# Attention values in halves of 64 queries, with the mixed corners corrected on quarters of the matmul array

## The chip, the core and the metric

The kernel runs on one NeuronCore of one Trainium2 chip. Its engines work side by side, each with its own queue: TensorE (PE in the profile, with PEld for loading its stationary operands, the "weights"), VectorE (DVE), ScalarE (ACT), GpSimd (POOL) and SyncE (SP). The last two mainly issue DMAs here. TensorE writes its results to PSUM, and VectorE and ScalarE read them from there.

The metric is the time of one launch in device microseconds (us). The median of three runs of the kernel before is 2309.34 us.

## The reference

One inference step of a two-layer decoder of width 2048 in fp32: a prompt of 1024 tokens, and eight single tokens that are decoded against caches. The first layer is a pooling mixer, the second one attention over a sliding window of 128 keys. The change touches the prompt's attention alone:

```python
def attn_core(q, k, v, q_pos, k_pos, sinks):
    s = jnp.einsum('...qkgd,...skd->...kgqs', q, k).astype(jnp.float32) * (HEAD_DIM ** -0.5)
    qp = q_pos[..., :, None]
    kp = k_pos[..., None, :]
    mask = (kp <= qp) & (qp - kp < WINDOW) & (kp >= 0)
    s = jnp.where(mask[..., None, None, :, :], s, NEG)
    ...
    p = jnp.exp(s - m)
    p = p / (jnp.sum(p, axis=-1, keepdims=True) + jnp.exp(sink - m))
    return jnp.einsum('...kgqs,...skd->...qkgd', p.astype(v.dtype), v)
```

Queries and keys go in blocks of 128 (`WINDOW`). Query number r of a block sees keys 0 to r of its own block and keys r+1 to 127 of the block before. So each query sees 128 keys, and for each key number k just one of the two blocks: its own where k <= r, else the one before. There are 32 query heads of width 64 on four key/value heads.

## The kernel before

**Steps.** Nearly all of the time goes into large products: the projections into and out of the two layers. Every fp32 operand is split into a rounded high part and a low remainder, and three matmuls (L684, L685, L686: high by high, high by low, low by high) make one product. Weights come in blocks of 128 x 1024; seven blocks in Strassen's scheme give two 128-row tiles of the result. One block is one *step*: 24 matmuls with 128 x 128 weights and 256 or 260 moving columns. (In a few places a step is half a unit of L712 to L714, 12 matmuls of 512 columns.)

**What sets the order.** The order of instructions on TensorE, VectorE and ScalarE is that of the source, written out by hand (`in_order`). A counter `i` goes up by one at the end of each step, and the attention's work hangs on it: `product(n, rank, go)` puts TensorE work at the end of step i+n, behind that step's 24 matmuls and sorted by rank; `at(n, go)` puts work of other engines there, behind the products. Between these, VectorE and ScalarE split the weights of coming steps (L505 on ScalarE, L520 on VectorE) and take results out of PSUM. `side_step` runs pieces of side work (layer norm, sums of weights), and passes where `lastO` says that the one-bank PSUM tile `pO` was taken just then.

**Attention.** The prompt goes in two chunks of 512 queries (c = 0, 1; chunk 1 also carries the eight decode tokens), that is NB = 4 query blocks each. `attend(c, t, ...)` is called for t = 0 to 15 in each chunk, 32 calls; one call does two heads (j = 0, 1, on partitions 0 to 63 and 64 to 127) for the four blocks. Its parts, some steps apart:

- `score` (PE, L1878): 32 fp32 matmuls with weights of 64 rows x 32 columns and 160 moving keys, into the four-bank PSUM tile `pS` (`self.S`, 2 x 1024 columns, one half for each j). The profile shows two records for each fp32 matmul.
- `select` (ACT, L1895) and `largest` (DVE, L1899) put the scores on the two key blocks into one 128 x 128 array per head and block; then come exponents, sums and the norm (L1914 to L1927).
- `turn` (PE, L1931): eight transposes into the first half of `pS`.
- `keep`: a copy `w` (ACT, L1940) and a masked copy `wp` (DVE, L1941) that keeps only entries with k > r.
- `values` (PE, L1955): for each block and head, all 128 keys of `w` against the own block's values `V[b + 1]`, and all 128 keys of `wp` against `Vd[b]`, the values of the block before less the own ones. These are 16 fp32 matmuls of 128 rows x 64 columns with 128 moving queries. They go to `pO` for t up to 12, to the second half of `pS` for t = 13 to 15.
- `gate` (DVE, L1964): the multiplication by the gate, out of PSUM, and a DMA of the result (POOL, L1967).

Calls start every seven steps. `phase_bi` gives each its place: `at` is the step of `score`, s1 the steps from there to `turn`, s2 = 2 those from `turn` to `values`; `gate` follows one step later. For most calls s1 is 12, so the values of one call fall to the end of the same step as the score of the next call but one, and rank puts the values first.

The decode tokens have small matmuls of their own: L2049 (weights of 64 rows x 128 columns, 8 moving columns) and L2089 (128 rows x 64 columns, 8 moving columns).

## Time and profile before

| | |
|---|---|
| three runs, median (lowest to highest) | 2309.34 us (2308.86 to 2309.92) |
| profiled execution: span from first to last instruction | 2308.8 us |
| TensorE busy | 2286.2 us (99%) |
| VectorE, ScalarE busy | 1943.5 us (84%), 1389.0 us (60%) |
| first score to last gate of the prompt's attention | 1148 to 2004 us of the span |

The profiled execution's own time is known by its span; the three runs lie 0.1 to 1.1 us above it.

A timeline row has start and duration in us, engine, line, operation, output and inputs, the part of the array in use (rows * columns), partitions x moving columns, and the number of records joined in the row. Matmuls are pipelined and their ends are modelled, so the distance from one start to the next says more of a matmul's cost than its duration. Matmuls on different parts of the array can run side by side: then several start within a few ns.

### The profile page before, as it was taken

The page shows a single profiled execution, that of the slowest core. Times are in us where ns is not written, and L with a number is a line of the kernel's source. Part 1 is how long each engine was busy: PE and PEld are TensorE (multiplying, and loading weights), DVE is VectorE, ACT ScalarE, POOL GpSimd, SP SyncE. Part 2 cuts the span into 40 slices and gives each one's busy share as a digit, 9 for nine tenths or more (in the row PEclk, how much of TensorE's full clock was granted, in tenths as well). Part 3 has the DMA queues.
Part 4 walks back from the last instruction along what each step waited for, and adds up shares of the span by engine and source line. Part 5 has one row for each costly group of instructions (what it writes and reads, how often), then busy time and mean ns, then how long its engine had stood idle before and what let it go on. Part 6 is the DMA issues. An engine that isn't in the chain of part 4 may idle for free.

```text
span 2308.8 us, 50518 instructions
## 1 busy us (share of the span) xinstructions
PE 2286.2 (99%) x20417; PEld 2216.1 (96%) x20417; DVE 1943.5 (84%) x2415; ACT 1389.0 (60%) x2547; POOL 191.1 (8%) x359
## 2 busy tenths in 40 slices
PE   9999999999999999999999999999999999999998
PEld 7999999999999999999889999999999999999998
DVE  8888889877868878998878888999877777888997
ACT  5544446544546556555576766785776678656665
POOL 0111100010000000000001111100000000000001
PEclk9999999999999999999999999999999999999999
DMA  7879679988989989999767667777787778799894
GB/s 260 284 245 315 229 252 327 317 302 300 303 304 323 339 293 321 317 385 359 235 241 249 224 237 243 263 273 233 236 261 233 248 241 293 245 365 360 286 342 149
DMA packets 246395, 648.31 MB, mean 281 GB/s; under 512 B 25201, under 2 KB 106001, under 8 KB 246161
## 3 DMA queue, kind: packets, MB, share of 16 engines
q1 hardware_dynamic: 204288, 493.13, 63.7%
q0 software_dynamic: 41872, 151.96, 17.0%
q8 instruction: 159, 2.61, 0.5%
q14 instruction: 76, 0.61, 0.1%
HBM read 463.00 MB, written 172.47 MB: 275 GB/s over the span
## 4 chain that ended last, share of the span: by engine, by line
PE 56%; DVE 1%; DMA 1%; ACT 0%; issue 0%; POOL 0%; SPq 0%; DVEq 0%; POOLq 0%
PE pD L684 15%; PE pD L686 14%; PE pD L685 14%; PE pO L1955 2%; PE pD L712 2%; PE pD L714 2%; PE pD L713 2%; PE pS L1878 2%; PE pS L1931 1%; DMA m<-in_wob 0%; PE pS L1955 0%; PE pO L684 0%; PE pO L685 0%; PE pO L686 0%; DVE m L520 0%; DMA m<-in_wib 0%
## 5 line engine op out<-in xcount | busy, mean ns | idle before, releaser
L684 PE MATMUL pD<-m,m 128*128 128x260 f32 (+1 forms) x5088 | 1441.1, 283 | 4.4 <-ACT pD L623 2.2
L686 PE MATMUL pD<-m,m 128*128 128x260 f32 (+1 forms) x5088 | 1434.0, 282 | 5.8 <-DVE m L520 5.8
L685 PE MATMUL pD<-m,m 128*128 128x260 f32 (+1 forms) x5088 | 1434.2, 282 | 0.0
L684 PEld LDWEIGHTS pD<-m,m 128*128 128x128 f32 x5088 | 958.9, 188 | 13.7 <-issue 6.2
L686 PEld LDWEIGHTS pD<-m,m 128*128 128x128 f32 x5088 | 959.5, 189 | 7.6 <-DVE m L520 7.4
L685 PEld LDWEIGHTS pD<-m,m 128*128 128x128 f32 x5088 | 958.6, 188 | 0.5
L520 DVE TENSOR_TENSOR m<-m,m 128x1024 fp32r<-128x1024 f32 x690 | 834.1, 1219 | 94.4 <-ACT m L505 37.9
L505 ACT CAST m<-m 128x1024 fp32r<-128x1024 f32 x690 | 720.6, 1049 | 247.5 <-DVE m L349 122.4
L349 DVE TENSOR_TENSOR m<-m,m 128x1024 f32<-128x1024 f32 x136 | 166.2, 1222 | 8.6 <-DMA m<-in_wia 5.6
L847 DVE TENSOR_TENSOR m<-m,m 128x1024 fp32r<-128x1024 f32 (+1 forms) x118 | 144.0, 1225 | 7.4 <-ACT m L838 5.8
L838 ACT CAST m<-m 128x1024 fp32r<-128x1024 f32 (+1 forms) x118 | 123.3, 1051 | 8.3 <-DVE m L520 3.9
L657 ACT COPY m<-pD 128x260 f32<-128x260 f32 (+1 forms) x88 | 32.9, 374 | 125.8 <-PE pD L686 125.6
L645 DVE TENSOR_TENSOR m<-pD,m 128x260 f32<-128x260 f32 (+1 forms) x92 | 38.3, 417 | 74.3 <-ACT pD L644 68.2
L1914 ACT ACTIVATE m<-m,sm 128x128 f32<-128x128 f32 x256 | 99.4, 392 | 0.0
L623 ACT ACTIVATE pD<-pD 128x260 f32<-128x260 f32 (+1 forms) x90 | 33.3, 370 | 98.8 <-PE pD L686 98.4
L1181 PE MATMUL pD<-m,m 128*128 128x260 f32 (+1 forms) x528 | 91.5, 323 | 0.0
L712 PE MATMUL pD<-m,m 128*128 128x512 f32 x224 | 89.1, 398 | 0.0
L714 PE MATMUL pD<-m,m 128*128 128x512 f32 x224 | 88.2, 394 | 0.0
L713 PE MATMUL pD<-m,m 128*128 128x512 f32 x224 | 88.1, 393 | 0.0
L1181 PEld LDWEIGHTS pD<-m,m 128*128 128x128 f32 x528 | 79.4, 188 | 8.2
L1927 ACT ACTIVATE m<-m,sm 128x128 f32<-128x128 f32 x256 | 81.9, 391 | 7.8 <-DVE sm L1922 7.2
L632 ACT COPY m<-pD 128x260 f32<-128x260 f32 (+1 forms) x92 | 34.4, 374 | 82.6 <-PE pD L686 82.4
(257 smaller groups left out, 2102.7 us busy)
## 6 DMA issues: line engine op xcount, KB each, us to landing
m<-in_wib SPq DMA_DIRECT2D x132, 512.0 KB
m<-in_wia SPq DMA_DIRECT2D x128, 512.0 KB
m<-swoa SPq DMA_DIRECT2D x64, 512.0 KB
swia<-m POOLq DMA_DIRECT2D x56, 512.0 KB, 4.8
m<-swia SPq DMA_DIRECT2D x56, 512.0 KB
m<-swob SPq DMA_DIRECT2D x56, 512.0 KB
m<-in_wob SPq DMA_DIRECT2D x52, 512.0 KB
m<-in_woa SPq DMA_DIRECT2D x48, 512.0 KB
```

The source lines that it names most:

```text
L349: self.nc.vector.tensor_add(s[out].a[:, :1024], s[x].a[:, :1024], s[y].a[:, :1024])
L505: self.nc.scalar.copy(hi.r[:, :1024], self.stream[self.cast].src().a[:, :1024])
L520: self.nc.vector.tensor_sub(lo.r[:, :1024], s.src().a[:, :1024], hi.a[:, :1024])
L684: nc.tensor.matmul(ps[:, :TH], wh[:, s], h, start=new and k == 0, stop=False, skip_group_check=on)
L685: nc.tensor.matmul(ps[:, :TH], wh[:, s], l, start=False, stop=False, skip_group_check=on)
L686: nc.tensor.matmul(ps[:, :TH], wl[:, s], h, start=False, stop=k == 7, skip_group_check=on)
L712: nc.tensor.matmul(ps[:], wh[:, s], h, start=par == 0 and k == 0, stop=False)
L713: nc.tensor.matmul(ps[:], wh[:, s], l, start=False, stop=False)
L714: nc.tensor.matmul(ps[:], wl[:, s], h, start=False, stop=par == 1 and k == 7)
L838: self.nc.scalar.copy(h.r[:, :n], s.a[:, :n])
L847: self.nc.vector.tensor_sub(l.r[:, :n], s.a[:, :n], h.a[:, :n])
L1181: nc.tensor.matmul(ps[:, : cs.stop - cs.start], ws[:, s], d[:, cs], start=f0 and k == 0, stop=l0 and k == 3,)
```

## The change

For queries 0 to 63 of a block (u = 0), keys 64 to 127 can only be those of the block before; for queries 64 to 127 (u = 1), keys 0 to 63 can only be the own ones. `values` now takes each half of 64 queries with all 128 keys against one block's values (`V[b]` for u = 0, `V[b + 1]` for u = 1). Only a corner of 64 keys by 64 queries is mixed, and is corrected with `Vd[b]` by matmuls of 64 rows x 64 columns: rows 0 to 63 with a turned sign for u = 0, rows 64 to 127 for u = 1. A new mask `mask2` (128 x 64, with the signs) takes the old one's place in `keep`, which now makes two multiplications of 64 partitions x 512 elements; `wp` takes half a memory slot. For the prompt's first block, whose block before is zero, the terms on it are left out.

Per call this is 32 fp32 matmuls (28 in chunk 0) with 64 moving queries in place of 16 with 128. The results always go to the second half of `pS`, u = 0 and u = 1 to different banks, and `gate` reads them with two multiplications of 128 x 256. Since the next score overwrites these banks, s1 becomes 10 in most calls: `turn`, `values` and `gate` come two steps earlier, the gate one step ahead of the step that ends with the next score. For the first block of chunk 0, `score` takes 32 to 128 moving keys in place of 160.

Cut from the diff below: the decode's small matmuls move to free columns of `pS`, the decode part of the value transposes (`dec`, `dec2`) goes two steps back, `use_four(True)` in the last phase from step 18 to 19, and `mask2` is passed in as an input.

```diff
@@ -79,7 +79,7 @@
 FILL = 4, 1, 1, 1, 1
 
 CLOSE, SPREAD = (1, 2, 3, 4, 5, 6, 7), (1, 2, 3, 5, 6, 7, 8)
-DEC_AT = (0, 1, 6, 6, 7, 8, 9, 10, 13, 13), (11, 11, 12, 12, 13, 14, 15, 16, 17, 17)
+DEC_AT = (3, 3, 6, 6, 7, 8, 9, 10, 13, 13), (11, 11, 12, 12, 13, 14, 15, 16, 17, 17)
 
 
 def in_order(tc):
@@ -1749,6 +1749,8 @@
             self.vd = B[:, 640:896]
             self.V = [A[:, 640:896]] + [C[:, b * 256 : (b + 1) * 256] for b in range(4)]
             self.Vd = [Dd[:, b * 256 : (b + 1) * 256] for b in range(4)]
+            self.mk2 = A[:, 896:960]
+            nc.sync.dma_start(self.mk2, self.io["mask2"])
             for k in self.kT:
                 nc.gpsimd.memset(k[:, 0:P], 0.0)
             self.at(4, lambda: nc.vector.memset(self.S[:, 1, :], 0.0))
@@ -1816,9 +1818,10 @@
             else:
                 s.free()
 
-        self.at(0, turn)
-        self.at(1, keep)
-        self.at(2, diff)
+        n = 2 if self.strassen else 0
+        self.at(n, turn)
+        self.at(n + 1, keep)
+        self.at(n + 2, diff)
         if T > TP:
 
             def dec():
...
@@ -1859,7 +1862,7 @@
         self.at(0, a)
         self.at(lag, b)
 
-    def attend(self, c, t, at, s1, s2, late=False, ticks=CLOSE):
+    def attend(self, c, t, at, s1, s2, ticks=CLOSE):
 
 
         nc = self.nc
@@ -1875,9 +1878,10 @@
                     r = slice(64 * j, 64 * j + 64)
                     for a in range(4):
                         h, k = 32 * a, b * P + 32 * a
+                        f = P - h if c == 0 and b == 0 else 0
                         nc.tensor.matmul(
-                            self.S[h : h + 32, j, b * 256 + h : b * 256 + h + 160], q[r, k : k + 32],
-                            self.kT[t // 8][r, k : k + 160], start=True, stop=True,
+                            self.S[h : h + 32, j, b * 256 + h + f : b * 256 + h + 160], q[r, k : k + 32],
+                            self.kT[t // 8][r, k + f : k + 160], start=True, stop=True,
                         )
             if lastq:
                 s.free()
@@ -1936,24 +1940,36 @@
         def keep():
 
 
-            x["w"], x["wp"] = self.mem.full(1024), self.mem.full(1024)
+            x["w"], x["wp"] = self.mem.full(1024), self.mem.half(512)
             nc.scalar.copy(x["w"].a[:, :1024], PT)
-            nc.vector.tensor_mul(
-                x["wp"].a[:, :1024].rearrange("p (i k) -> p i k", k=P),
-                PT.rearrange("p (i k) -> p i k", k=P),
-                cst[:, None, K_MP + 1 :].to_broadcast([P, 8, P]),
-            )
+            for u in range(2):
+                r = slice(64 * u, 64 * u + 64)
+                nc.vector.tensor_mul(
+                    x["wp"].a[r, :512].rearrange("p (i k) -> p i k", k=64),
+                    PT.rearrange("p (i k) -> p i k", k=P)[r, :, r],
+                    self.mk2[r, None, :].to_broadcast([64, 8, 64]),
+                )
 
         def values():
-            o = x["o"] = self.S[:, 1, :512] if late else self.psO()
+
             for b in range(NB):
-                bs = slice(b * P, (b + 1) * P)
-                for n, (V, p) in enumerate(((self.V[b + 1], x["w"].a), (self.Vd[b], x["wp"].a))):
+                bs = slice(64 * b, 64 * b + 64)
+                first = c == 0 and b == 0
+                todo = [] if first else [(0, slice(0, P), self.V[b])]
+                todo += [(1, slice(0, P), self.V[b + 1])]
+                todo += [(0, slice(0, 64), self.Vd[b])] + ([] if first else [(1, slice(64, P), self.Vd[b])])
+                for n, (u, r, V) in enumerate(todo):
+                    whole = r.stop - r.start == P
                     for j in range(2):
                         vs = slice((2 * (t // 8) + j) * HD, (2 * (t // 8) + j + 1) * HD)
-                        ms = slice((2 * b + j) * P, (2 * b + j + 1) * P)
+                        i = 2 * b + j
+                        if whole:
+                            p = x["w"].a[:, i * P + 64 * u : i * P + 64 * u + 64]
+                        else:
+                            p = x["wp"].a[r, 64 * i : 64 * i + 64]
                         nc.tensor.matmul(
-                            o[64 * j : 64 * j + 64, bs], V[:, vs], p[:, ms], start=n == 0, stop=n == 1
+                            self.S[64 * j : 64 * j + 64, 1, 512 * u + bs.start : 512 * u + bs.stop], V[r, vs], p,
+                            start=whole or first, stop=not whole or first, skip_group_check=True,
                         )
             x["w"].free()
             x["wp"].free()
@@ -1961,9 +1977,13 @@
         def gate():
             a = self.ao[c, t] = self.mem.half(T)
             z, j = self.sg.pop((c, t))
-            nc.vector.scalar_tensor_tensor(
-                a.a[:, :TP], x["o"][:, :TP], 0.5, z.a[:, j * T : j * T + TP], op0=ALU.mult, op1=ALU.mult
-            )
+            four = lambda v, u: v.rearrange("p (b u k) -> p u b k", u=2, k=64)[:, u]
+            for u in range(2):
+                nc.vector.scalar_tensor_tensor(
+                    four(a.a[:, :TP], u),
+                    self.S[:, 1, 512 * u : 512 * u + 256].rearrange("p (b k) -> p b k", k=64), 0.5,
+                    four(z.a[:, j * T : j * T + TP], u), op0=ALU.mult, op1=ALU.mult,
+                )
             nc.gpsimd.dma_start(self.act["o", c][:, t, :TP], a.a[:, :TP])
             if c == 1:
                 self.ao.pop((c, t)).free(True)
...
@@ -2047,12 +2067,12 @@
                 for j in range(2):
                     r = slice(64 * j, 64 * j + 64)
                     nc.tensor.matmul(
-                        self.S[:, j, 8 * b : 8 * b + 8], dk[r, b, :], self.qd[pr][r, b, :], start=True, stop=True
+                        self.S[:, j, 256 + 8 * b : 264 + 8 * b], dk[r, b, :], self.qd[pr][r, b, :], start=True, stop=True
                     )
 
         def s1():
             for j in range(2):
-                nc.vector.tensor_copy(st[:, 64 * j : 64 * j + 64], self.S[:, j, :64])
+                nc.vector.tensor_copy(st[:, 64 * j : 64 * j + 64], self.S[:, j, 256:320])
             ks.free(True)
 
         def s2():
@@ -2140,7 +2160,7 @@
                     nc.scalar.copy(s.a[:, :T], ps[:])
                     self.gate_done(c, t, s, 1)
 
-                self.attend(c, t, 9, 13 if t <= 2 * ps[-1] else 8, 2)
+                self.attend(c, t, 9, 12 if t <= 2 * ps[-1] else 8, 2)
                 self.unit(q_done)
                 if t == 2 * ps[-1] - 1:
                     self.x_begin(nxt)
@@ -2161,10 +2181,10 @@
                 self.at(2, lambda p=p: self.dec_keys(p // 4))
             for n in range(2):
                 t = t0 + n
-                at, s1, ticks = (12 + 7 * n, {12: 11, 13: 9}.get(t, 12), SPREAD) if t < 14 else (
-                    11 + 7 * n, {14: 10, 15: 8}[t], CLOSE
-                )
-                self.attend(c, t, at, s1, 2, t > 12, ticks)
+                at, s1, ticks = 12 + 7 * n, 8 if t == 15 else 10, SPREAD if t < 14 else CLOSE
+                if ps[0] and t == 2 * ps[0]:
+                    at, s1 = at + 1, s1 - 1
+                self.attend(c, t, at, s1, 2, ticks)
             if p == ps[-1]:
                 self.x_begin(nxt)
                 if c == 1:
...
@@ -2402,7 +2422,9 @@
     for g, w in enumerate(WINDOWS):
         rc[:, g * NST : (g + 1) * NST] = w / np.minimum(w, np.arange(NST) + 1.0)
     mask = np.arange(P + 1)[None, :] <= np.arange(P)[:, None]
-    return np.eye(P, dtype=f), mask.astype(f), rc
+    low = np.arange(64)[:, None] <= np.arange(64)[None, :]
+    two = np.concatenate([-low.astype(f), f(1) - low.astype(f)])
+    return np.eye(P, dtype=f), mask.astype(f), rc, two
 
 
 def kernel(**inputs):
```

On TensorE, around the values of the first call of chunk 1: the shapes are output partitions x columns, `m_2191` is `w`, `m_2192` is `wp`, `m_1544` holds `V`, `m_1545` holds `Vd`, `pO` and `pS` are the PSUM tiles; the row of L1878 is the score of the call with t = 2. Before:

```order
L686 MATMUL pD_19920<-m_2070_18742,m_2184_19986 128x260
L1955 MATMUL pO_20106<-m_2191_20068,m_1544_13091 64x128 x2
L1955 MATMUL pO_20106<-m_2192_20069,m_1545_13092 64x128 x2
...
L1955 MATMUL pO_20106<-m_2191_20068,m_1544_13091 64x128 x2
L1955 MATMUL pO_20106<-m_2192_20069,m_1545_13092 64x128 x2
L1878 MATMUL pS_13088<-m_1542_13089,m_2162_19721 32x160 x32
L684 MATMUL pD_19873<-m_2078_18787,m_2185_19988 128x260
```

After (L1970 is `values`; `m_2177` is `w`, `m_2173` is `wp`, `m_1542` holds `V` of the block before):

```order
L686 MATMUL pD_20078<-m_2010_18474,m_2170_20121 128x260
L1970 MATMUL pS_13088<-m_2177_20202,m_1542_13089 64x64 x2
L1970 MATMUL pS_13088<-m_2177_20202,m_1544_13091 64x64 x2
L1970 MATMUL pS_13088<-m_2173_20170,m_1545_13092 64x64 x4
L1970 MATMUL pS_13088<-m_2177_20202,m_1544_13091 64x64 x4
L1970 MATMUL pS_13088<-m_2173_20170,m_1545_13092 64x64 x4
...
L1970 MATMUL pS_13088<-m_2177_20202,m_1544_13091 64x64 x4
L1970 MATMUL pS_13088<-m_2173_20170,m_1545_13092 64x64 x4
L684 MATMUL pD_20117<-m_2046_18748,m_2171_20123 128x260
```

The matmuls of one shape became runs of two shapes in turn, four of each per block, and no score follows them. That score now stands two steps further on, alone between matmuls of the large products:

```order
L686 MATMUL pD_20126<-m_2065_18908,m_2179_20209 128x260
L1882 MATMUL pS_13088<-m_1542_13089,m_2155_19927 32x160 x32
L684 MATMUL pD_20078<-m_2071_18958,m_2180_20211 128x260
L685 MATMUL pD_20078<-m_2077_19001,m_2180_20211 128x260
L686 MATMUL pD_20078<-m_2071_18958,m_2183_20281 128x260
```

On VectorE, from the masked copy to the gate of the same call and to the next copy of scores. Before:

```order
L1941 TENSOR_TENSOR m_2192_20069<-pS_13088,cst 128x1024
L1921 TENSOR_TENSOR sm_19902<-sm_19902,sm_19901 128x8
L1922 RECIPROCAL sm_19902<-sm_19902 128x8
L645 TENSOR_TENSOR m_2187_20036<-pD_19911,m_2179_19950 128x260
L520 TENSOR_TENSOR m_2194_20078<-m_2176_19913,m_2190_20042 128x1024
L650 TENSOR_TENSOR m_2187_20036<-pD_19920,m_2179_19950 128x260
L520 TENSOR_TENSOR m_2197_20162<-m_2180_19952,m_2195_20080 128x1024
L1964 SCALAR_TENSOR_TENSOR m_2199_20190<-pO_20106,m_2137_19429 128x512
L453 TENSOR_TENSOR m_2186_20033<-m_2186_20033 128x512
L520 TENSOR_TENSOR m_2203_20205<-m_2183_19984,m_2198_20164 128x1024
L1899 COPY_PREDICATED m_2200_20197<-cst,pS_13088 128x1024
```

After (L1947 is the masked copy, L1982 the gate, L1903 the copy of scores; L1740 and L1851 are the rotary embedding of queries):

```order
L1947 TENSOR_TENSOR m_2173_20170<-pS_13088,m_1542_13089 64x512 x2
L520 TENSOR_TENSOR m_2179_20209<-m_2156_19929,m_2176_20176 128x1024
L1740 TENSOR_TENSOR m_2155_19927<-m_2155_19927,m_1546_13097 128x1040
L1740 TENSOR_TENSOR m_2168_20111<-m_2168_20111,m_1546_13097 128x1040
L1851 TENSOR_TENSOR m_2155_19927<-m_2155_19927,m_2168_20111 128x1040
L1855 COPY area<-m_2155_19927 128x8x2
L520 TENSOR_TENSOR m_2183_20281<-m_2165_20072,m_2180_20211 128x1024
L1982 SCALAR_TENSOR_TENSOR m_2173_20170<-pS_13088,m_2131_19641 128x4x64 x2
```

The masked copy and the gate became two rows each, and the rotary embedding now stands between them; the next copy of scores comes eleven rows behind the gate instead of three.

## What is predicted

> **What bounds the kernel now.** First the page: busy shares, then the chain that ended last.
>
> ```profile
> PE 2286.2 (99%) x20417; PEld 2216.1 (96%) x20417; DVE 1943.5 (84%) x2415; ACT 1389.0 (60%) x2547; POOL 191.1 (8%) x359
> PEclk9999999999999999999999999999999999999999
> PE 56%; DVE 1%; DMA 1%; ACT 0%; issue 0%; POOL 0%; SPq 0%; DVEq 0%; POOLq 0%
> ```
>
> TensorE is busy to 99% at its full granted clock, and of what the chain names nearly all is TensorE. But matmuls overlap in these records, so a busy share alone would hide a wait. So next, for the stretch with the attention, the sums by stretch and TensorE's waits:
>
> ```profile
> 1116.00:2006.00 890.00, 887.16 (x9297) 848.41 (x9296) 750.38 (x945) 618.14 (x1412) 76.47 (x141) 1.00 0.74 247
> PE pD L684 <- ACT m L657: 1.7, 1, 1.7
> ...
> PE pS L1878 <- DVE m L1848: 0.4, 1, 0.4
> ```
>
> (Columns of the first row: length, then busy time of PE, PEld, DVE, ACT, POOL, the clock, DMA share, GB/s.) TensorE waits 2.8 us of 890 (890.00 less 887.16), at a few single places. So every ns that the change adds to TensorE's queue, or takes from it, shows in the total, and work on other engines shows only if it makes TensorE wait. Last, the timeline of TensorE around one call's values and the next score:
>
> ```profile
> 1355.12 0.28 PE L685 MATMUL pD<-m,m 128*128 128x256 f32 x1
> 1355.23 0.28 PE L686 MATMUL pD<-m,m 128*128 128x256 f32 x1
> 1355.44 1.97 PE L1955 MATMUL pO<-m,m 128*64 128x128 f32 x32
> 1357.34 1.32 PE L1878 MATMUL pS<-m,m 64*32 64x160 f32 x64
> 1358.59 0.39 PE L684 MATMUL pD<-m,m 128*128 128x256 f32 x1
> 1358.81 0.28 PE L685 MATMUL pD<-m,m 128*128 128x256 f32 x1
> ```
>
> Ordinary matmuls start 0.12 us apart (1355.12, 1355.23). Wherever the part of the array in use changes, more time passes: 0.21 us to the first record of the values, 0.22 us from the first ordinary matmul behind the score to the second. The values hold the queue from 1355.44 to 1357.34, 1.90 us for 32 records.
>
> **What a change of shape costs.** It is not the new line or a semaphore, since a change of line without a change of shape costs nothing. The transposes follow in step:
>
> ```profile
> 1372.75 0.28 PE L686 MATMUL pD<-m,m 128*128 128x256 f32 x1
> 1372.87 1.03 PE L1931 MATMUL pS<-cst,m 128*128 128x128 f32 x8
> ...
> 1747.23 0.28 PE L686 MATMUL pD<-m,m 128*128 128x260 f32 x1
> 1747.44 1.96 PE L2049 MATMUL pS<-area,m 64*128 64x8 f32 x32
> ...
> 1795.57 0.28 PE L686 MATMUL pD<-m,m 128*128 128x260 f32 x1
> 1795.77 1.10 PE L2089 MATMUL pO<-m,m 128*64 128x8 f32 x32
> 1796.44 0.44 PE L2089 MATMUL pO<-m,m 128*64 128x8 f32 x10
> 1796.81 0.39 PE L684 MATMUL pD<-m,m 128*128 128x260 f32 x1
> 1797.03 0.28 PE L685 MATMUL pD<-m,m 128*128 128x260 f32 x1
> ```
>
> 0.12 us to the transposes (same 128*128), but 0.21 us where only the rows change (L2049, 64*128) and 0.20 us where only the columns do (L2089, 128*64). The same shape of weights as in the values, with 8 moving columns, also gives what a record costs when its moving part is nearly nothing: the five pairs of the row x10 (two places of the array, two records at a time, each 0.20 long) start 0.06 us apart, (0.44 - 0.20) / 4. That is the pace of loading 64 columns of weights. The last pair starts at 1796.44 + 0.24 = 1796.68, and 0.13 us pass until the next shape.
>
> For the values as they are, two more narrow looks at the timeline, at the begin of the run quoted above and at the end of another:
>
> ```profile
> 1355.44 0.44 PE L1955 MATMUL pO<-m,m 128*64 128x128 f32 x4
> ...
> 1516.56 0.28 PE L686 MATMUL pD<-m,m 128*128 128x260 f32 x1
> 1516.77 1.97 PE L1955 MATMUL pS<-m,m 128*64 128x128 f32 x32
> 1518.35 0.39 PE L1955 MATMUL pS<-m,m 128*64 128x128 f32 x4
> 1518.67 0.39 PE L684 MATMUL pO<-m,m 128*128 128x260 f32 x1
> 1518.89 0.29 PE L685 MATMUL pO<-m,m 128*128 128x260 f32 x1
> ```
>
> A record is 0.28 long, so the second pair starts 0.44 - 0.28 = 0.16 us behind the first: a weight load that nothing hides (0.05) and one pair's moving part (0.11). Further pairs come 0.11 us apart (0.39 - 0.28): here the moving columns set the pace. The last pair starts at 1518.46, and 0.21 us pass until the next shape, the moving part of 0.11 and 0.09 to 0.10 more. Check: 0.16 + 14 x 0.11 + 0.20 = 1.90 us, as measured.
>
> **The change, part by part.**
>
> *Values.* With 64 moving columns the moving part of a pair is half of 0.11, 0.055 us, just under the loading pace of 0.06; I take 0.058 per further pair. The first pair of a run of one shape then takes 0.05 + 0.055, about 0.11 (rows: 0.16 with 128 moving columns; with 8, 1796.68 - 1795.77 = 0.91 less 14 x 0.06 leaves 0.07). The hold behind the last pair is 0.055 + 0.095 = 0.15 (rows: 0.20 and 0.13). Per block there are now two runs. The whole-key one has 8 records on two places, 4 deep: 0.11 + 2 x 0.058 + 0.15 = 0.38 us. The corner has 8 records on four places, 2 deep if all four run side by side: 0.11 + 0.15 = 0.26 us. That is 0.64 us a block and 2.54 us a call in chunk 1, against 1.90: +0.64. In chunk 0 the first block has half of the terms, 0.26 + 0.26 = 0.52, so 2.43: +0.53. Sixteen calls each: 16 x 1.17 = +18.7 us. The work in the array itself shrinks (24 deep x 0.058 = 1.4 us against 1.7); the seven new changes of shape in a call cost more than that. No row has the new pair of shapes, 128*64 to 64*64. I price it like the others because the rows show the hold for rows alone, for columns alone, and for both. The bounds, with every first pair and hold at the cheaper row (0.07, 0.13), are 0.07 + 0.12 + 0.13 = 0.32 and 0.20: 2.08 us a call, +0.18 in chunk 1 and +0.06 in chunk 0 (its first block 0.40 for 0.52), +4 us in all; at the dearer (0.16, 0.20) 0.48 and 0.36: 3.36 us and 3.24, +45 us. I keep the middle, since 64 lies about halfway between 8 and 128 moving columns.
>
> [...]
>
> *Values apart from the score.* A row more for a score that stands alone:
>
> ```profile
> 1284.80 0.28 PE L686 MATMUL pD<-m,m 128*128 128x256 f32 x1
> 1285.00 1.32 PE L1878 MATMUL pS<-m,m 64*32 64x160 f32 x64
> 1286.25 0.38 PE L684 MATMUL pD<-m,m 128*128 128x256 f32 x1
> 1286.47 0.28 PE L685 MATMUL pD<-m,m 128*128 128x256 f32 x1
> ```
>
> From the last ordinary matmul to the second one after it: values alone 1518.89 - 1516.56 = 2.33, score alone 1.67, both in one go 1358.81 - 1355.23 = 3.58 us. Apart they hold two ordinary distances of 0.12 more, which are no loss: 2.33 + 1.67 - 0.24 - 3.58 = 0.18 us. In the orders, 22 calls have their values directly ahead of a score before, and none after (one is ahead of a decode matmul): 21 x 0.18 = +3.8 us.
>
> *Score of chunk 0's first block.* Its longest place has 128 moving keys in place of 160, two records deep. With the pace of 0.11 for 128, and a quarter more for 160, that is 2 x 0.027 us a call: 16 x 0.054 = -0.9 us.
>
> *VectorE.*
>
> ```profile
> L1899 DVE COPY_PREDICATED m<-cst,pS 128x1024 f32<-128x1024 int32 x32 | 42.8, 1337 | 7.8 <-ACT m L1895 4.7 <-PE pS L2049 2.7 <-issue 0.4
> L1941 DVE TENSOR_TENSOR m<-pS,cst 128x1024 f32<-128x1024 f32 x32 | 39.1, 1222 | 38.3 <-ACT m L1940 32.3 <-PE pD L685 6.0
> L453 DVE TENSOR_TENSOR m<-m 128x512 f32<-128x512 f32 x56 | 38.3, 684 | 0.0
> L458 DVE TENSOR_TENSOR m<-m 128x256 f32<-128x256 f32 x56 | 23.8, 425 | 1.9
> L1964 DVE SCALAR_TENSOR_TENSOR m<-pO,m 128x512 f32<-128x512 f32 x26 | 17.8, 686 | 4.6 <-PE pO L1955 4.6
> ```
>
> The masked copy, two of 512 elements (0.684 each) for one of 1.222: +0.15 us. The gate, two of 256 (0.425) for 0.686: +0.16. Over 32 calls that is +10 us of VectorE, which is busy 750 of 890 us here: hidden behind TensorE, and +10 us at most if that cover were gone. What can reach TensorE are three waits. Values wait for the masked copy, two steps (5.7 us) behind the transposes as before; its lateness is the same but for the 0.15 us, and TensorE waited so close to nothing that I put +0.5 us on the few calls that were just in time (bounds 0 and 32 x 0.15 = 5). The transposes now come three steps behind the next score, not five, and need L1899 to be done; the score now waits for the gate, two steps behind the values. The rotary embedding (L1740, L1851) and two L520 stand ahead of the gate, five instructions of some 1.22 us (a full-width one as in L1941's row): 6 us. They are counted from the masked copy, which runs a step or more ahead of the values, and two steps pass after these. The latest L1899 that no decode matmul held up is this one:
>
> ```profile
> 1791.46 1.32 PE L1878 MATMUL pS<-m,m 64*32 64x160 f32 x64
> ...
> 1798.80 1.31 DVE L1899 COPY_PREDICATED m<-cst,pS 128x1024 f32<-128x1024 int32 x1
> ```
>
> It ends at 1800.11, 7.3 us behind its score's end, and three steps are 3 x 24 x 0.12 = 8.6 us. So I cost both waits at nothing; half a step (1.4 us) in every call would be the dear end, +45 us. In front of the SP queue stands one more small load (`mask2`), and POOL's DMA of the result is issued earlier; neither is on TensorE's path.
>
> Sum: 18.7 + 3.8 - 0.9 + 0.5 = +22.1 us, so a span of 2308.8 + 22.1 = 2330.9. The median of the runs is 0.5 us above the span: 2331.4.
>
> **Rivals.**
>
> *No hold between 128\*64 and 64\*64* (the other side). The columns in use stay 64, and whole-key runs and corners might follow each other as one run. Then a call is one run 24 deep, 0.11 + 22 x 0.058 + 0.15 = 1.54 us, in chunk 0 22 deep, 1.42: -0.36 and -0.48, 16 x -0.84 = -13.4. With +3.8, -0.9 and +0.5: -10.0, 2299.3 us. In the sum, a change inside a call costs (2.54 - 1.54) / 7 = 0.14 us; the sign turns where it costs 22.1 / (32 x 7) = 0.10 us less, 0.04. For it: no row shows this pair. Against it: L2049's row changes rows alone and pays in full. [...]
>
> *Corners one row half after the other.* If the two corners of a block don't run side by side, a corner is 4 deep: + 0.12 us a block, 0.46 a call: +14 us, 2345. For it: no 64*64 rows here. Against it: the score's 64 records take 1.25 us, 0.02 each, which only places side by side allow.
>
> *A new wait of TensorE on VectorE* at the transposes or the next score, as above: a third to a whole step per call for half the calls (16 x 1 to 2.85 us), +16 to +45 us on top, 2347 to 2377. For it: two steps less in the chain of a call, and the rotary embedding ahead of the gate. Against it: waits of 2.8 us in 890 and VectorE idle for 140.
>
> **How the numbers follow.** Forecast 0.70, own range 2319 to 2342; no hold 0.10; corners in turn 0.09; new waits 0.08; the remaining 0.03 for effects that cancel to near nothing. The likeliest gives 2331.4. (The dear end of the values, 2358, would need a first pair as long as with 128 moving columns, against the half of it that has to be moved.) From 2317, the cheap end, to 2347 the range leaves out the no-hold case, the near-nothing one, most of the new waits and a little of the forecast's ends, 0.2 together. A change within 0.2% (4.6 us) is about what can't be told from none. Slower than that: forecast, corners, waits, 0.87; within it 0.03; faster 0.10.
>
> **What will show it.** Right: in a call's timeline the values take about 2.5 us, in eight short runs by turns of 128*64 and 64*64, and some 0.15 us pass between the last start of one and the first of the next; scores stand alone between ordinary matmuls; TensorE's waits stay at a few us; VectorE has 10 us more. Wrong: the values take 1.4 to 1.6 us with even distances (no hold); corner runs are as long as whole-key ones (corners in turn); the transposes or the score have long idle times ahead of them that end with VectorE (new waits).

## The result, and the profile after

| | median | runs | against before |
|---|---|---|---|
| before, same chip | 2309.32 us | 2308.86 to 2309.92 | |
| changed | 2337.02 us | 2335.46 to 2340.63 | 1.0123 (95% interval 1.0110 to 1.0135) |

The change makes the kernel slower by 27.7 us, 1.2%. Predicted were +22.1 us and 2331.4 us, with a range of 2317 to 2347. The profiled execution after has a span of 2333.9 us.

The same views as before, now of the changed kernel. First the page: busy time, and clock by slices.

```profile
PE 2310.7 (99%) x21313; PEld 2225.1 (95%) x21313; DVE 1955.7 (84%) x2479; ACT 1385.9 (59%) x2547; POOL 192.7 (8%) x359
PEclk9999999999999999999999999999999999999999
```

VectorE has 12.2 us more (1955.7 against 1943.5), where +10 was predicted; TensorE is busy to 99% as before. Next the sums over the attention (length, then busy time of PE, PEld, DVE, ACT, POOL, the clock, DMA share, GB/s), and TensorE's waits in it (total, times, longest).

```profile
1116.00:2031.00 915.00, 911.64 (x10175) 856.80 (x10173) 761.05 (x1005) 613.74 (x1410) 75.57 (x139) 1.00 0.73 240
```

```profile
PE pD L686 <- DVE m L520: 0.7, 2, 0.5
PE pD L684 <- ACT m L657: 0.6, 1, 0.6
PE pS L1970 <- DVE m L1947: 0.6, 2, 0.3
...
PE pS L1804 <- DVE m L1982: 0.4, 1, 0.4
```

The stretch is 25 us longer than the one summed before (915 against 890), with about the same ordinary matmuls in it. TensorE waits 3.4 us of it (915.00 less 911.64), against 2.8 before. So the added time is not waiting. It is TensorE's own, and the timeline of one call's values (chunk 1) shows where. The last three rows show the first runs of the call singly, which the timeline otherwise joins into the one row of 64 records.

```profile
1649.98 0.28 PE L685 MATMUL pD<-m,m 128*128 128x260 f32 x1
1650.10 0.28 PE L686 MATMUL pD<-m,m 128*128 128x260 f32 x1
1650.31 2.70 PE L1970 MATMUL pS<-m,m 128*64 128x64 f32 x64
1652.94 0.39 PE L684 MATMUL pD<-m,m 128*128 128x260 f32 x1
1653.17 0.28 PE L685 MATMUL pD<-m,m 128*128 128x260 f32 x1
...
1650.31 0.45 PE L1970 MATMUL pS<-m,m 128*64 128x64 f32 x8
1650.69 0.34 PE L1970 MATMUL pS<-m,m 64*64 64x64 f32 x8
1650.97 0.45 PE L1970 MATMUL pS<-m,m 128*64 128x64 f32 x8
```

The call holds the queue from 1650.31 to 1652.94, 2.63 us; before it was 1.90. A whole-key run takes 1650.69 - 1650.31 = 0.38 us and a corner 1650.97 - 1650.69 = 0.28. A whole-key record is 0.22 long, so the last one of the first run starts at 1650.31 + 0.45 - 0.22 = 1650.54, and 0.15 us pass until the corner's first. The corner's last starts at 1650.69 + 0.34 - 0.22 = 1650.81, and again 0.15 to 0.16 us pass. Eight runs make seven such changes inside a call, and 0.15 us passes at each, in which no other matmul starts (a *hold*, below).

The score that the values no longer precede now stands alone:

```profile
1658.57 0.28 PE L685 MATMUL pD<-m,m 128*128 128x260 f32 x1
1658.68 0.28 PE L686 MATMUL pD<-m,m 128*128 128x260 f32 x1
1658.90 1.32 PE L1882 MATMUL pS<-m,m 64*32 64x160 f32 x64
```

It pays 0.22 us on the way in (1658.68 to 1658.90), about as a lone score did before (0.20).

To put every part in one account, the distances from each matmul's start to the next one's were summed over both traces, by what the two matmuls are. From first to last matmul the sums are 2299.1 and 2324.1 us: +25.0.

| sum of distances, us | before | after | difference |
|---|---|---|---|
| between records of one call's values | 54.49 | 77.22 | +22.7 |
| from the values to what follows | 6.95 | 4.75 | -2.2 |
| from an ordinary matmul to a score | 2.44 (10 times) | 7.08 (32 times) | +4.6 |
| between records of one score | 32.70 | 31.85 | -0.85 |
| from an ordinary matmul to value transposes and values | 7.04 | 8.59 | +1.55 |
| between ordinary matmuls | 2150.41 | 2149.84 | -0.6 |

The rest is under 0.6 us; of the +1.55, 0.2 stood behind values before. The last row hides two things that cancel: 22 distances fewer (22 x 0.12 = -2.6) and 22 more slow first distances behind a change of shape (0.23 in place of 0.12, +2.4).

### The profile page after: what moved, and what is told of

It is laid out like the page before. It is cut to its first block, busy times and chain, and to the rows that moved or that the text cites. A ratio compares the mean times of both kernels' runs of the same rounds, so it can differ in the third digit from the quotient of the medians.

```text
span 2333.9 us, 52367 instructions
## 1 busy us (share of the span) xinstructions
PE 2310.7 (99%) x21313; PEld 2225.1 (95%) x21313; DVE 1955.7 (84%) x2479; ACT 1385.9 (59%) x2547; POOL 192.7 (8%) x359
## 5 line engine op out<-in xcount | busy, mean ns | idle before, releaser
L684 PE MATMUL pD<-m,m 128*128 128x260 f32 (+1 forms) x5088 | 1443.3, 284 | 3.9 <-ACT pD L623 2.4
L686 PE MATMUL pD<-m,m 128*128 128x260 f32 (+1 forms) x5088 | 1433.8, 282 | 5.6 <-DVE m L520 5.4
L684 PEld LDWEIGHTS pD<-m,m 128*128 128x128 f32 x5088 | 958.5, 188 | 15.0 <-issue 6.3
L686 PEld LDWEIGHTS pD<-m,m 128*128 128x128 f32 x5088 | 958.7, 188 | 8.1 <-DVE m L520 8.1
L644 ACT COPY pD<-pD 128x260 f32<-128x260 f32 (+1 forms) x78 | 28.0, 359 | 126.5 <-PE pD L686 126.3
L1918 ACT ACTIVATE m<-m,sm 128x128 f32<-128x128 f32 x256 | 99.3, 392 | 0.0
```

The source lines that it names most:

```text
L684: nc.tensor.matmul(ps[:, :TH], wh[:, s], h, start=new and k == 0, stop=False, skip_group_check=on)
L686: nc.tensor.matmul(ps[:, :TH], wl[:, s], h, start=False, stop=k == 7, skip_group_check=on)
L1918: nc.scalar.activation(x["s3"][:, i, :], x["s3"][:, i, :], AF.Exp, bias=nm[:, i : i + 1], scale=0.125, accum_out=rs[:, i : i + 1],)
```

## The experiments

The theory: each change of shape inside a call costs about 0.14 us of TensorE's time, in which little runs. Its main rivals: the price is that of the records (32 fp32 matmuls a call in place of 16), or it comes from the new places and the waits that they make, or from the further input.

Differences below are of medians, against the kernel before on the same chip in the same comparison (2308.3 to 2310.2 us). By them the changed kernel stands at +27.7.

### All whole keys first, then all corners

```diff
-            for b in range(NB):
-                todo = [] if first else [(0, slice(0, P), self.V[b])]
-                todo += [(1, slice(0, P), self.V[b + 1])]
-                todo += [(0, slice(0, 64), self.Vd[b])] + ([] if first else [(1, slice(64, P), self.Vd[b])])
...
+            todo = [(b, u, slice(0, P), self.V[b + u]) for b in range(NB) for u in range(2) if c or b or u]
+            todo += [
+                (b, u, slice(64 * u, 64 * u + 64), self.Vd[b]) for b in range(NB) for u in range(2) if c or b or not u
+            ]
...
```

> The changed kernel with the values of a call in another order: first the whole-key matmuls of all four blocks (128*64), then all corners (64*64). The same matmuls, one change of shape inside a call in place of seven. Theory (each change of shape holds TensorE's queue by some 0.15 us and hides no weight load): a call's values take 0.11 + 14 x 0.0585 + 0.15 = 1.08 us for the whole-key part and 0.11 + 6 x 0.0585 + 0.17 = 0.63 us for the corners, 1.71 us in place of 2.63 in chunk 1 and 1.59 in place of 2.49 in chunk 0; over 32 calls -29 us, a median of 2308 us, about the time before the change. Rival (64 records in place of 32 cost their own time each, whatever their order): values stay at 2.6 us and the median at 2337.

Measured: 2309.26 us (2306.04 to 2313.14), 1.0002 (0.9993 to 1.0012), +0.8 us. The same instructions in another order take back nearly the whole loss. Inside the values TensorE spent 47.79 us, 29.4 less than the changed kernel: for 192 changes of shape fewer (six in each call) that is 0.153 us each. The count of records is the same, so it isn't the records. In this order the values are even 6.7 us shorter than the old ones. That this doesn't show as a gain has two reasons: the separated scores, and waits. In the waits of this kernel, the value transposes of chunk 1 now stand out:

```profile
PE pS L1804 <- DVE m L1982: 2.1, 1, 2.1
PE pD L684 <- ACT m L657: 1.7, 1, 1.7
PE pD L672 <- ACT m L657: 1.5, 1, 1.5
```

TensorE comes to them earlier and waits 2.1 us for the last gate of chunk 0 (0.4 in the changed kernel). This profiled execution, the slowest of the ten (2313.14 us), also has two stretches of 3.41 us at half the granted clock in the attention, the first of them 1.4 us behind this wait.

### Whole rows in place of corners

```diff
...
-                todo += [(0, slice(0, 64), self.Vd[b])] + ([] if first else [(1, slice(64, P), self.Vd[b])])
+                todo += [(0, "wp", self.Vd[b])] + ([] if first else [(1, "wp", self.Vd[b])])
...
-    two = np.concatenate([-low.astype(f), f(1) - low.astype(f)])
+    two = np.zeros((P, P), f)
+    two[:64, :64], two[64:, 64:] = -low.astype(f), f(1) - low.astype(f)
```

The corners' weights are filled up with zeros to 128 rows, so that all 32 matmuls have one shape. `wp` is of full size again, and for its memory slots fewer weights are loaded ahead where less than five slots are free.

> The corners as matmuls over all 128 rows, with zeros in the masked copy outside the corner: as many matmuls as in the changed kernel, in the same order, with more work in the array, but all of one shape (128*64). Theory (the change of shape costs, not the count): values take 0.11 + 30 x 0.0585 + 0.16 = 2.02 us in chunk 1 and 1.79 us in chunk 0, in place of 2.63 and 2.49; over 32 calls -21 us, a median of 2316 us. Rival (the count of records costs): no gain, 2337 us. The same rule on loads as in the kernel with the old values.

Measured: 2319.80 us (2317.42 to 2321.65), 1.0045 (1.0027 to 1.0063), +11.3 us. Timeline of a call in chunk 1:

```profile
1636.83 0.28 PE L686 MATMUL pD<-m,m 128*128 128x260 f32 x1
1637.04 2.08 PE L1963 MATMUL pS<-m,m 128*64 128x64 f32 x64
1639.06 0.39 PE L684 MATMUL pD<-m,m 128*128 128x260 f32 x1
```

As many records as in the changed kernel, each corner now over twice the rows, and the call takes 2.02 us in place of 2.63. Inside the values it is 55.89 us, 21.3 less; 21 were expected. Here more work of one shape is cheaper than less work of two. So the rival of the records falls a second time. Another rival falls with it: that a corner is held up because it adds to columns of PSUM that were written just before. Here the sums go to the same columns in the same order, and no hold is left. The time itself misses the expected 2316 us by 4. The trace has waits ahead of the transposes (1.7 us), the value transposes (1.5) and one call's values (1.0) that the changed kernel has not or has shorter; the next kernels share them.

### The new places with the old values

```diff
...
-                todo += [(1, slice(0, P), self.V[b + 1])]
...
+                for n, (V, p) in enumerate(((self.V[b + 1], x["w"].a), (self.Vd[b], x["wp"].a))):
...
+                            o[64 * j : 64 * j + 64, bs], V[:, vs], p[:, ms], start=n == 0, stop=n == 1
...
```

> The new places (transposes, values and gate two steps earlier, values apart from the score, result in the second half of pS) with the old values: 16 matmuls of 128 rows x 64 columns with 128 queries, the old mask, one gate multiplication. Theory (the new shapes cost 20.5 us, the places about 4): values take 1.9 us a call again, the median is 2337 - 20.5 = 2316 us. Rival (the earlier places make TensorE wait for VectorE, and that is what was lost): TensorE's waits grow and the median stays above 2325. To fit into memory fewer weights are loaded ahead where under five slots are free.

> The new places of the change (the steps at which transposes, values and gate stand, values apart from the score) with the old values: 16 matmuls of 128 moving queries, the old mask, one gate. The decode's small matmuls go to columns 512 to 575 of each half, so that nothing is overwritten. Theory: what is left of the change are the separation (21 x 0.18 = 3.8 us predicted, 4.3 found), the shorter score (-0.9) and about 1 us of waits: +4 to +5 us over the kernel before. The earlier kernel of this kind came out at +11.9 us, with some 23 us of single TensorE waits of over 0.3 us in all; if that stands again here, the new places cost about 7 us more once the old full-size memory slot for the masked copy is kept, by waits for memory slots, and the separation is not more than what it was.

In the first of the two, the decode's small matmuls overwrite one call's result ahead of its gate, which changes the output and not the instructions. Measured: 2320.34 us (2317.75 to 2322.85), 1.0051 (1.0035 to 1.0067), +11.9; and 2321.64 us (2316.98 to 2324.01), 1.0054 (1.0040 to 1.0067), +13.3. The values are back at 54.24 us, as before the change, and yet the 2316 us expected of the first were missed by 4 us, and the +4 to +5 of the second by more than 8. The waits of the second one:

```profile
PE pS L1804 <- DVE m L1969: 2.2, 1, 2.2
PE pD L684 <- ACT m L657: 1.7, 1, 1.7
PE pS L1935 <- DVE m L2068: 1.6, 1, 1.6
PE pS L1960 <- DVE m L1945: 1.0, 2, 0.8
```

They are single waits, 6.5 us in all, where the changed kernel has 1.6 for the same pairs. The first is that of the grouped kernel. That the longer values of the changed kernel cover it, because TensorE comes later, fits, but no run tests it by itself. To see what the rule on loading, which these kernels and the one with whole rows share, has to do with it, the changed kernel was run with that rule alone:

```diff
-        if getattr(self, "ph", "") == "bi1" and len(self.mem.whole()) < 3:
+        if getattr(self, "ph", "") in ("bi0", "bi1", "bo0") and len(self.mem.whole()) < 5:
```

> The changed kernel with the rule alone that the kernels with old values and with whole rows needed for their larger masked copy (fewer weights loaded ahead where less than five memory slots are free). Those kernels stand some 8 us above the sum of their separated scores (+4.2) and shorter first score (-0.9), by single waits of TensorE. If the rule makes these waits, this kernel lies 5 to 8 us over the changed one, near 1.0145 times the kernel before, with TensorE waits of 8 us more; if they come from the places together with the shorter values, it stays at 1.0112 to 1.0123.

Measured: 2337.90 us (2337.28 to 2341.31), 1.0126 (1.0109 to 1.0143), +28.1. It stays at the changed kernel's time, but not quite without a trace, for two of the four waits are there:

```profile
PE pS L1970 <- DVE m L1947: 1.7, 3, 1.0
PE pS L1935 <- DVE m L2083: 1.7, 1, 1.7
```

So the 1.6 us ahead of the transposes (L1935) belong to the rule. The 0.8 us ahead of the values (L1960 above) seem to as well: 0.8 to 1.0 us stand ahead of the twelfth call's values in all four kernels with the rule. In the changed kernel they don't, though run once more it has 1.0 us ahead of another call. By the account of distances, the trace of these old values at the new places is 10.7 us longer than that of before: +4.2 for the separation, -0.9 for the first score, +5.6 for the ways into the transposes (1.8, the rule's wait), the value transposes (2.3) and the values (1.5), and some 2 us between ordinary matmuls. Of the 2.6 us that remain of +13.3, some 1.6 are what the profiled execution of before was longer than its median (an estimate, see below); more was not tried.

### The masks in one input

```diff
-            nc.sync.dma_start(self.mk2, self.io["mask2"])
+            nc.sync.dma_start(self.mk2, self.io["mask"][:, P + 1 :])
...
```

> The changed kernel with its new mask in 64 further columns of the old mask's input, so that the kernel has no input more than before. In the changed kernel the time of a run lies 2.1 to 2.4 us above its span, before it was about 0.5. If the further input costs that time outside the span, the median falls by 1.5 to 1.9 us to 2335.3 and the span stays; if not, it stays at 2337.

> The changed kernel itself, word for word, as the control for the three beside it. Expected: 1.0123 times the time of the kernel before, as in the first comparison (about 28 us more), TensorE's waits in the attention again some 3 to 4 us of 915, values 77 us from start to start. Rival: the 3 us by which the kernel with the masks in one input lay lower was an effect of that input; then this one stands at +28, not at +25. If this one too comes out near +25, the chip or the day made the difference.

Measured with one input: 2333.94 us (2331.85 to 2335.42), 1.0109 (1.0093 to 1.0125), +25.5. The changed kernel once more: 2334.62 us (2333.98 to 2335.05), 1.0112 (1.0098 to 1.0126), +26.3. So the further input has no part in it that could be told, and the changed kernel itself comes out at +26.3 in one comparison and at +27.7 in another.

### Twice as many changes of shape

```diff
                 todo = [] if first else [(0, slice(0, P), self.V[b])]
-                todo += [(1, slice(0, P), self.V[b + 1])]
-                todo += [(0, slice(0, 64), self.Vd[b])] + ([] if first else [(1, slice(64, P), self.Vd[b])])
+                todo += [(0, slice(0, 64), self.Vd[b]), (1, slice(0, P), self.V[b + 1])]
+                todo += [] if first else [(1, slice(64, P), self.Vd[b])]
```

> The changed kernel with the same matmuls in another order: in each block whole keys of half 0, its corner, whole keys of half 1, its corner. So there are 16 runs of one shape in a call in place of 8 (15 to 14 in chunk 0, whose first block keeps its two), with 4 records each, and no instruction more. Theory (each change of shape costs about 0.14 us, whichever side it comes from): four runs of 0.106 + 0.150 = 0.256 us are 1.02 us a block in place of 0.656, +0.37 us for 112 blocks: +41 us over the changed kernel, values 77 + 41 = 118 us from start to start. Rival (the price is that of a record, 0.02 us each): no difference, 77 us. Rival (a change to the corner is dear, the one back is cheap, or the reverse): the distances at the two kinds of change differ by more than 0.05 us, with the same sum.

Measured: 2405.43 us (2404.86 to 2409.71), 1.0423 (1.0409 to 1.0437), +97.1: 71 us over the changed kernel in the same comparison, not 41. Inside the values the expectation holds: 120.61 us against 77.23, +43.4. (A call has 15 changes in chunk 1 but 12 in chunk 0, where whole keys of two blocks come to stand side by side: 208 changes more in all, where the expectation counted two a block, 224.) In a call of chunk 1:

```profile
1675.85 0.34 PE L1970 MATMUL pS<-m,m 128*64 128x64 f32 x4
1676.12 0.33 PE L1970 MATMUL pS<-m,m 64*64 64x64 f32 x4
...
1675.85 4.28 PE L1970 MATMUL pS<-m,m 128*64 128x64 f32 x64
1680.07 0.39 PE L684 MATMUL pD<-m,m 128*128 128x260 f32 x1
```

A run of four records takes 0.27 us, little less than one of eight, and the call 4.22 us in place of 2.63. For both ways of the change the distance is the same to 0.01 us, so neither side is the dear one. But 27 us are left, and nearly all of them lie in the ordinary matmuls: 2173.6 us between them against 2147.0. The waits are not longer:

```profile
PE pD L684 <- ACT m L657: 0.6, 1, 0.6
PE pS L1970 <- DVE m L1947: 0.6, 2, 0.3
```

The timeline behind a call of chunk 0 shows them at half pace, and the sums by stretch (same columns as above; the clock is the 1.00 or 0.51 ahead of the last two numbers) name the reason:

```profile
1363.04 3.61 PE L1970 MATMUL pS<-m,m 64*64 64x64 f32 x56
1366.58 0.55 PE L684 MATMUL pD<-m,m 128*128 128x256 f32 x1
1366.92 0.42 PE L685 MATMUL pD<-m,m 128*128 128x256 f32 x1
1367.14 0.41 PE L686 MATMUL pD<-m,m 128*128 128x256 f32 x1
...
1369.70 0.41 PE L686 MATMUL pD<-m,m 128*128 128x256 f32 x1
...
1370.10 0.28 PE L685 MATMUL pD<-m,m 128*128 128x256 f32 x1
```

```profile
1366.40:1366.80 0.40, 0.40 (x5) 0.33 (x6) 0.40 (x1) 0.32 (x1) 0.00 (x0) 0.81 0.00 0
1366.80:1370.10 3.30, 3.30 (x16) 3.30 (x17) 2.69 (x6) 0.72 (x1) 0.98 (x2) 0.51 0.05 19
1370.10:1372.00 1.90, 1.90 (x19) 1.90 (x18) 0.31 (x1) 0.70 (x2) 0.40 (x2) 1.00 0.95 371
...
1680.07:1683.48 3.41, 3.41 (x32) 3.41 (x29) 1.60 (x5) 0.18 (x1) 0.56 (x1) 1.00 0.60 152
```

For some 3.3 us behind these values the granted clock is 0.51, and the matmuls start 0.21 us apart in place of 0.12. The last row stands behind the call of chunk 1 above: there the clock stays at 1.00. Such a stretch follows 15 of the 32 calls here (the expectation below counts 16), and none in the two profiles of the changed kernel. The busy row says 100% all the while; only the clock column and the distances tell. Some 2.6 of the 27 us belong to another stretch of the same kind, at the end of a wait of 2.8 us after the attention.

The trace also shows which calls are followed. Each stretch at half clock in this kernel's attention lasts 3.413 us or twice that (6.827, after three calls), and their starts lie whole multiples of 3.413 us apart, to 0.01 us. Carried on over all 32 calls, this grid of 3.413 us sorts them without an exception: the 15 calls that fill at least 3.18 us of one grid step have half clock from the next step on (which can begin up to 1.6 us before the call's end), and the 17 that fill at most 3.11 us of any step have not. In the changed kernel a call of 2.6 us can't fill that much of a step.

### The values in two parts

```diff
...
+        if s1 == 10:
+            s1 = 9
+            self.product(at + s1 + s2, 1, lambda: values((0, 1)))
+            self.product(at + s1 + s2 + 1, 1, lambda: values((2, 3)))
+            s2 = 3
+        else:
+            self.product(at + s1 + s2, 1, values)
         self.product(at + s1, 0, turn)
         self.at(at + s1 + 1, keep)
-        self.product(at + s1 + s2, 1, values)
```

Once on the doubled order and once, as the control, on the changed kernel. In both, the earlier transposes overwrite a part of the next call's scores ahead of the masked copy, which changes the output and not the instructions.

> The order of the kernel with doubled changes of shape, but in 25 of the 32 calls the values come in two parts of two blocks each, with a whole step of ordinary matmuls between them (the transposes one step earlier, the gate one step later). The doubled order took 71 us more than the changed kernel where 41 were expected: 43 us inside the values, and some 25 us in the ordinary matmuls behind them, which ran at half pace for about 2.8 us after 16 of the calls. Theory: what halves the clock is that the array is thinly used for 4 us on end; two parts of 2 us, shorter than the 2.6 us after which the changed kernel keeps its pace, leave no such stretch. Then about 22 us go away and the splitting costs 25 x 0.24 = 6 us: 2388 us, and 43 us over the kernel below with the same split. Rival: the clock follows the number of changes of shape, or the work as a whole; then the half-pace stretches stay and it is 65 to 71 us over the kernel below.

> The changed kernel with the same split of the values into two parts, as the control for the kernel above: each split costs one more way in and out (0.21 from the last ordinary matmul to the first of the values, 0.15 behind the last, less an ordinary distance of 0.12: 0.24 us), 25 times: +6 us, 2341 us where the changed kernel has 2334.6. If the transposes a step earlier or the gate a step later make TensorE wait, it is more, by what TensorE's waits show.

Measured: 2410.98 us (2409.28 to 2414.84), 1.0440 (1.0423 to 1.0458), +100.8, and for the control 2370.20 us (2369.19 to 2371.51), 1.0260 (1.0245 to 1.0276), +60.0. As times, both numbers of the theory fail: the split cost not 6 us but 34, mostly because the values now come before their copies are ready. The waits, the same in both kernels:

```profile
PE pS L1970 <- ACT m L632: 13.7, 10, 2.0
PE pS L1970 <- DVE m L1947: 6.3, 9, 1.2
```

With the same waits in the two, their difference still tells theory and rival apart: 40.8 us, where the theory had 43 and the rival 65 to 71. Inside the values it is 115.57 - 73.76 = 41.8 us, and between ordinary matmuls 2156.0 against 2155.2, next to nothing. In these two traces the doubled changes cost the clock nothing once they don't stand in one piece. The grid agrees: a part of 2.1 us can't fill 3.18 us of a step. Of the seven calls that are still whole in the doubled kernel, the one that fills 3.19 us of a step is followed by half clock, and the six that fill at most 2.62 are not. What this does not show is a time without those stretches: the doubled kernel has five stretches at half clock in the attention and its control six, most of them behind waits of 1 to 2 us ahead of a part.

### Grouped, with the value transposes a step later

```diff
-        n = 2 if self.strassen else 0
+        n = 3 if self.strassen else 0
         self.at(n, turn)
```

This is the grouped kernel with the masks in one input besides.

> The grouped order (all whole-key matmuls of the four blocks, then all corners) with the transposes of chunk 1's values one step later, and the masks in one input. In the grouped kernel's profile TensorE waited 2.4 us ahead of these transposes for the last gate of the call before, and its clock was at half for 3.4 us soon after. Theory: with that wait gone, 1.5 to 4 us less than the grouped kernel: 0.9983 to 0.9995 of the kernel before, faster by 1 to 4 us at best. Rival: the wait is found again a few places on (at the matmuls that wait for the copy of the values, or at the next score), and the time is the grouped kernel's, 1.000.

Measured: 2307.72 us (2305.22 to 2310.02), 0.9996 (0.9987 to 1.0005), -0.6 us. The wait at L1804 (2.1 us, where the expectation has 2.4) is gone and nothing has come in its place:

```profile
PE pD L672 <- ACT m L657: 1.4, 1, 1.4
PE pD L684 <- ACT m L657: 1.1, 1, 1.1
PE pS L1969 <- DVE m L1947: 0.6, 2, 0.3
PE pS L1882 <- DVE m L1982: 0.3, 1, 0.3
```

```profile
1632.50 0.28 PE L686 MATMUL pD<-m,m 128*128 128x260 f32 x1
1632.70 1.78 PE L1969 MATMUL pS<-m,m 128*64 128x64 f32 x64
1634.41 0.39 PE L684 MATMUL pD<-m,m 128*128 128x260 f32 x1
```

A call takes 1.71 us, less than the old 1.90. It beats the changed kernel by 27 us. Against the kernel before, and against the grouped one, it can't be told from no change. From first to last matmul its trace is 4.7 us shorter than that of before: values and holds save some 9 us, the first score 0.9, and the separation gives 4.4 back, with some small waits. About 1.6 of the 4.7, by the estimate below, is the long profiled execution of before; the other 3 lie just at the end of the interval (-3.0 to +1.2 us).

## Why the prediction was right, and where it fell short

The direction, the mechanism and the range were right; the size was 5.6 us short.

- **The hold between 128\*64 and 64\*64.** Predicted 0.15 us, though no row showed the pair; measured 0.15 both ways. A change of shape was put at 0.14 us; the grouped order gives 0.153, and the doubled one 0.14 (43.4 us, less 1.3 in calls that were already at half clock, less 112 blocks with two pairs each that no longer run beside another, 224 x 0.058, over 208 further changes). The first rival, no hold, is out: the values would have been 1.54 us a call, not 2.63.
- **The values, +18.7.** Mis-sized: +20.5 us (22.7 inside, less 2.2 behind them). The whole-key run is exact, 0.38 us. The step that failed is the corner's 0.26: it is 0.275, because the four places start one behind the other, about 0.007 us apart, where the sum had them start at once. So a call took 2.63 and not 2.54 us in chunk 1, 2.50 and not 2.43 in chunk 0. That the corners would run one half after the other, the second rival, is out: a corner would then be as long as a whole-key run.
- **Values apart from the score, +3.8.** 22 lone scores more cost 4.64 on the way in, -2.6 and +2.4 between ordinary matmuls: +4.4 us.
- **The score of the first block, -0.9.** Measured -0.85.
- **Waits, +0.5.** About +1.35 on the ways into the values and the value transposes (the 1.55 of the table less the 0.2 that stood behind values before). As idle time over the whole stretch it is 0.6 more (3.4 against 2.8). The third rival, TensorE waiting for VectorE at the transposes or the next score, did not come: the wait of L1804 for the gate is 0.4 us and stands alone. The experiments show that this was nearer than the prediction had it: with shorter values the same place waits 2.1 us.
- **VectorE, +10, hidden.** +12.2, hidden.
- **The time that stands around the span, +0.5.** This step failed. It compared the profiled span with the times of other executions. In each run for which both are known, the time is 1.7 to 3.6 us above its own span, 2.1 in the middle (2336.28 and 2333.9 for the changed kernel; 2307.74 and 2305.6 for a run of the kernel before). By that the profiled execution of before, with a span of 2308.8, itself took about 2310.9 us, 1.6 more than the median; this is an estimate, since its own time is not known. It has longer waits on L686 and L684 (2.7 and 1.7 us, against 0.7 and 0.6 after), and 3.41 us at half clock from near the end of the first of them on, which the changed kernel's trace has not. A sum made on it starts too high, and leaves out what the other runs don't wait for.

So by its own terms the sum of +22.1 was short by 1.8 us in the values, 0.6 in the separation and about 1 in the waits, and about 0.5 too high elsewhere (between ordinary matmuls, a term that it did not have). That makes +25, which is what the two traces show from first to last matmul. The other 1.3 to 2.7 us to the medians (+26.3 and +27.7) are of the size of what the choice of one execution to stand for before makes.

## What to carry to other kernels

On a TensorE that is never idle, count the changes of shape as you count instructions: here each cost 0.14 to 0.15 us, as much as two and a half more pairs of these small matmuls (0.058 each), and putting all matmuls of one shape first took back some 26 us without removing one. A long stretch of thin work can cost again behind it: when a call grew from 2.6 to 3.5 us and more, the clock fell to half for 3.4 us or more at the end of 15 of the 32 calls, which no busy column shows. Take the time above the span, and the waits, from more than one execution before building a sum of a few us on them.

## What was not expected of the hardware

- **The clock falls behind work, not only behind waits.** Behind a wait it stands in the trace of before: 3.41 us at half clock, from near the end of a wait of 2.46 us on. In the doubled kernel, 15 of 32 calls of 3.5 us (chunk 0) and 4.2 us (chunk 1), in which TensorE's records leave no gap, were followed by 3.41 or 6.83 us at half clock: just those that filled at least 3.18 us of a step of the grid of 3.413 us on which these stretches start. Calls of 2.5 to 2.6 us were not, nor the 3.15 us of values and score together before, which fall just short of 3.18. The grid was read off the finished traces and not forecast, and the split kernels had stretches at half clock of their own, so that the stretch in one piece is the cause is borne out but not proven. What in the thin work brings the clock down, the traces don't show.
- **Places start one behind the other.** Four matmuls on four quarters start 0.007 us apart (the first records of a corner at 0, 0.007, 0.013 and 0.020 us), a pair 0.006 to 0.007.
- **More array work, less time.** With zeros filled in, the corners cover twice the rows, and a call takes 2.02 us in place of 2.63.
